# Earlier weight loads, squares by rows, contiguous weights and tokens, and later value products in a one-layer attention trunk

## The chip, the core and the metric

The kernel runs on one core of a Trainium2 chip. Its engines work in parallel, each through its own instructions in order: PE (TensorE, matrix products; PEld is its weight load), ACT (ScalarE), DVE (VectorE), POOL (GpSimd) and SP (SyncE), which here only issues transfers. All transfers of the program go through SP's one queue and are carried out by 16 DMA engines. The metric is device time in microseconds (us) of one execution.

## The reference, cut to what matters

```python
def project(h, g_norm, w_in, b_f):
    u = rmsnorm(h, g_norm) @ w_in              # 1024 -> 4104 columns
    qa, ka, va, ga, qb, kb, vb, gb, fl = jnp.split(u, ...)   # 512 each, fl 8
    logf = log_sigmoid(fl + b_f)
...
# heads A (8): stick-breaking attention      heads B (8): softmax with a forgetting decay
#   w = sigmoid(z) * prod of later sigmoid(-z)      p = softmax(q k / 8 + c_q - c_k)
mixed = concat([oa * silu(ga), ob * silu(gb)])
h = h + mixed @ w_out;   y = rmsnorm(h, final_g)
```

There are 2048 prompt tokens, 16 meta tokens before them and 32 tokens of a running stream (2096 rows of 1024), whose 32 tokens also attend to a cache of 2048 keys. Keys, values and log forgets are outputs too. All is float32.

## The kernel before

Products keep float32 precision by splitting each factor into a high and a low part (ACT copies the high part, `sub` or a multiply-subtract makes the low one on DVE, or on POOL for streamed tokens) and adding three products (`mm3`, L261 to L263). A projection is cut into **sections** of 512 columns: `v1`, `k1`, `q1` for heads B, then `k0`, `v0`, `q0`, `g0` for heads A and the gates, `g1`, and the two halves of the output product (`ob`, `oa`). A section has two **units** of 256 columns (`load_unit`): each is loaded in two halves of 512 KB into raw tiles (`wraw`, `wraw2`), then split into `whi`, `wlo`, eight row blocks a unit. A unit's steps (loads, splits) lie in a list `prep`, from which `tick` takes one at a time while a section's products are written down (`every` 2: at every second tick).

The time line has three stages. **First**, v1, k1 and q1 run alone on PE from tokens that stay resident. `feed` brings the 17 blocks of 128 tokens (transposed, `x_T`, 512 KB), splits them and finds each token's norm: ACT squares the block, POOL adds the squares in three instructions, a PE product sums over partitions (`ptx`, `root`), and `newton` (DVE, ACT) makes `r_all`, by which v1's results `vt` are scaled. 40 products without use (`WARM`) run before the weights are there. **Second**, attention of heads B (`fx_main`) is interleaved with a filler: k0, v0, q0, g0, then g1 and the output products. There tokens are streamed a chunk at a time (`stream`: load `xw` from `x_K`, copy, subtract on POOL), the next chunk during the current one, at the ticks. **Third**, attention of heads A (`sb_main`): per step a score tile (`a`, ACT sigmoids, a DVE scan, a POOL product), for an earlier step four transposes `pta` on PE copied by ACT to `pth`, and after four of them the eight value products `four_pv` (`pv_half`, L701), `poa`. They are put off by one step:

```python
pend.append((t + (1 if f.__name__ == "four_pv" else 2), f))
```

Instructions are written in this order, but a scheduler that plans with costs of its own then orders each engine's queue; only q1's PE and DVE instructions are pinned to the written order. What is printed below is what the diff touches.

Of the kernel before, what the change touches and what calls it, by code (L numbers as in the profile page):

```python
# [16 lines left out]
NX = 2048  # L17
# [34 lines left out]
NW = 9  # L52
FINE = ('k1', 'q1')
# [25 lines left out]
def trunk_step_kernel(ctx, tc, x_all, x_T, x_K, ca_kT, ca_v, cb_kT, cb_v, cb_lfT, norm_g, w_in, b_f, w_out,  # L79
# [77 lines left out]
    def constants():  # L157
        mf = stage("mf", F32, "sg")[:, :SEC]
        dma(mf, mask_c)
        nc.vector.tensor_copy(masks16, mf)  # L160
        sf = stage("sf", F32, "sg")
# [8 lines left out]
        one = stage("one", F32, "sg")[0:8, :SEC]  # L170
# [6 lines left out]
    def load_unit(src, cols, kt, nm, g=None, raw1=None):  # L177

        hi = w_p.tile([128, KT * 264], F32R, tag="whi", name=f"whi{nm}")
        lo = w_p.tile([128, KT * 264], F32R, tag="wlo", name=f"wlo{nm}")  # L180
        hi, lo = ([a[:, k * cols:(k + 1) * cols] for k in range(kt)] for a in (hi, lo))
        raw = {}

        def load(i):
            if i and raw1 is not None:
                raw[i] = raw1
# [10 lines left out]
        def split(i, ks=range(kt // 2)):  # L197
            for k in ks:
# [12 lines left out]
        if nm[:2] in FINE:  # L211
            part = [[lambda i=i: load(i)] + [lambda: None] * NOP + [lambda i=i, k=k: split(i, (k, k + 1)) for k in (0, 2)]
                    for i in range(2)]
            return (hi, lo), part[0] + part[1]
        return (hi, lo), [lambda: load(0), lambda: split(0), lambda: load(1), lambda: split(1)]
# [17 lines left out]
    class Units:  # L233
        every = 2
# [3 lines left out]

        def prepare(self, u):
            un, steps = self.unit(u)  # L240
            self.un.append(un)
            self.prep += steps
# [37 lines left out]
    class SecT(Units):  # L280
        def __init__(self, nm, base, chunks, src, acc, evac, ahead=None, lead=0):
            super().__init__()
            self.nm, self.base, self.chunks, self.src, self.acc, self.evac = nm, base, chunks, src, acc, evac
            self.ahead, self.lead = ahead, lead
            self.every = 1 if lead else 2
# [3 lines left out]
        def unit(self, u):  # L289
            b = self.base + 256 * u  # L290
            return load_unit([w_in[:, b:b + 256]], 256, KT, f"{self.nm}{u}", g_col)
# [5 lines left out]
        def run(self):  # L297
# [13 lines left out]
            for c, (a, n, us) in enumerate(seq):  # L311
# [8 lines left out]
                for i, (p, b, m) in enumerate(order):  # L320
                    if self.next and c == half and i == len(order) // 2:
# [55 lines left out]
    class SecV(Units):  # L377
        def __init__(self, s, chunks, src, acc):
            super().__init__()
            self.s, self.chunks, self.src, self.acc, self.raw1 = s, chunks, src, acc, None  # L380
            self.next = None

        def unit(self, u):
            s = self.s
            base = SECS * s + 2 * SEC
            cols = [w_in[:, base + 256 * u:base + 256 * u + 256]]
            if s and u == 0:
                cols.append(w_in[:, 2 * SECS:2 * SECS + 8])
            return load_unit(cols, 264 if s and u == 0 else 256, KT, f"v{s}{u}", g_col, self.raw1 if u == 0 else None)
# [23 lines left out]
        def run(self):  # L413
# [9 lines left out]
            for i, (a, n) in enumerate(chunks):  # L423
# [10 lines left out]
                for j, (t, u) in enumerate(order):  # L434
                    if self.next and i + 1 == len(chunks) and j == len(ts):
# [169 lines left out]
    def stream(nm, a, n):  # L605
        t = {}
        eng = nc.gpsimd
        n0 = n if n <= XC else 256
# [34 lines left out]
        if n0 < n:  # L643
            steps += halve(lambda: raw(1), lambda: part("xh", 1), lambda: part("xl", 1), pairs(KT, KT), eng)
# [7 lines left out]
        def at_(tag):  # L652
            return lambda k, c, m: (part(tag)[:, k, c - a:c - a + m] if c - a < n0 else
                                    part(tag, 1)[:, k, c - a - n0:c - a - n0 + m])
# [132 lines left out]
    class SbSet:  # L787
# [40 lines left out]
        def b(self, i):  # L828
# [13 lines left out]
            wt = f2k("pth", f"pth{gr.nm}_{kc}_{j}", 4)  # L842
# [170 lines left out]
    def sb_main():  # L1013
# [45 lines left out]
        while t < len(first_a) or second:  # L1059
# [280 lines left out]
    def out_b():  # L1340
# [17 lines left out]
        for j, c in enumerate(seq):  # L1358
# [12 lines left out]
            for i, ((a, r, mh, ml), u) in enumerate(order):  # L1371
                if j == 0 and i == len(order) // 2:
                    ob.ready()
                if j == 4 and i == len(order) // 2:
# [68 lines left out]
    k0 = SecT("k0", SEC, CH_K, stream, ps_a, evac_k(0))  # L1443
# [311 lines left out]
```

## Time and profile before

| | |
|---|---|
| median of 3 runs | 1927.68 us (1919.27 to 1928.73) |
| the profiled execution's own time | 1933.34 us |
| its span, first to last instruction | 1931.3 us |
| PE busy | 1871.1 us, 97% |
| DVE, POOL, ACT busy | 1268.2, 1142.8, 1052.9 us |
| mean granted TensorE clock | 0.985 |
| transfers | 330.69 MB, 171 GB/s |

The span is what the profile divides into busy and idle time; the execution's own time is 2.0 us longer, and this execution lay 5.7 us above the median. A PE that is idle waits for data; a PE that is busy at a granted clock of 0.5 works at half speed (1.2 of 2.4 GHz).

### The profile page before, as it was taken

The numbers are of one execution on the slowest core, as the hardware profiler recorded it, in microseconds if no ns is written. First come the engines' busy times: TensorE is split into PE (matmuls) and PEld (weight loads), VectorE is DVE, ScalarE is ACT, GpSimd is POOL, SyncE is SP. The second block draws the span as 40 slices with busy tenths as digits, with TensorE's granted clock in tenths as the row PEclk, the third lists the DMA queues.
The fourth block names the chain that finished last, engine by engine and source line by source line (L and its number), as shares of the span: only waits on it lengthen the run. The fifth ranks groups of instructions, "written<-read, shape, count | busy, mean of one in ns | idle before, by whom it ended". The sixth has DMA issues, their size and how long they took to land.

```text
span 1931.3 us, 35966 instructions
## 1 busy us (share of the span) xinstructions
PE 1871.1 (97%) x12154; PEld 1474.2 (76%) x12154; DVE 1268.2 (66%) x2387; ACT 1052.9 (55%) x2291; POOL 1142.8 (59%) x1691
## 2 busy tenths in 40 slices
PE   7999999999999999999999999999998999999998
PEld 6999998676776777767777788777876766766676
DVE  5436336765575445566566467788878897778776
ACT  5541213453454454645355577787766777777742
POOL 3500002786777777767786676667766777667400
PEclk8999999999999999999999999999999999999999
DMA  7656757566566454667667545475656554534454
GB/s 160 186 140 148 182 138 189 146 185 163 165 167 162 123 163 137 189 194 213 202 216 213 180 142 185 139 230 167 207 179 196 169 187 136 165 112 143 154 201 175
DMA packets 260431, 330.69 MB, mean 171 GB/s; under 512 B 46685, under 2 KB 195382, under 8 KB 254102
## 3 DMA queue, kind: packets, MB, share of 16 engines
q1 hardware_dynamic: 260246, 328.39, 57.9%
q8 instruction: 96, 1.57, 0.3%
q14 instruction: 89, 0.73, 0.1%
HBM read 211.61 MB, written 116.68 MB: 170 GB/s over the span
## 4 chain that ended last, share of the span: by engine, by line
PE 76%; DVE 9%; DMA 7%; ACT 3%; issue 2%; POOL 2%; SPq 1%; DVEq 0%; POOLq 0%; ACTq 0%
PE pob L701 6%; PE poa L701 5%; PE pta L840 5%; PE sb L1151 3%; PE psTq L261 3%; PE smb L1123 3%; PE psv L261 3%; PE sb L1152 3%; PE psTq L263 3%; PE psTq L262 3%; PE psTk L261 3%; PE psv L262 3%; PE psv L263 3%; PE psTk L263 3%; PE psTk L262 3%; PE sa L781 3%
## 5 line engine op out<-in xcount | busy, mean ns | idle before, releaser
L753 POOL TENSOR_TENSOR wa<-wa,mba 128x512 f32<-128x512 f32 (+1 forms) x320 | 367.2, 1150 | 153.9 <-DVE wa L747 132.2
L1165 POOL TENSOR_TENSOR accb<-accb,pfb 128x512 f32<-128x512 f32 (+1 forms) x256 | 297.6, 1162 | 122.3 <-ACT pfb L1155 106.5
L747 DVE TENSOR_TENSOR_SCAN wa<-sa,wa,ones_r 128x512 f32<-128x512 f32 x192 | 244.3, 1278 | 48.1 <-ACT sa L744 34.4
L1155 ACT ACTIVATE pfb<-sb 128x512 f32<-128x512 f32 (+1 forms) x320 | 175.2, 552 | 182.8 <-PE sb L1152 175.1
L1131 DVE TENSOR_REDUCE mxb<-smb 128x1 f32<-128x512 f32 (+1 forms) x320 | 195.2, 613 | 101.2 <-PE smb L1123 96.7
L843 ACT COPY ptha<-pta 128x512 f32<-128x512 f32 (+1 forms) x320 | 167.1, 526 | 94.5 <-PE pta L840 91.4
L743 ACT ACTIVATE mba<-sa 128x512 f32<-128x512 f32 (+1 forms) x320 | 174.4, 545 | 20.0 <-POOL wa L753 16.2
L840 PE MATMUL pta<-ident,wa 128*128 128x128 f32 x1088 | 174.2, 275 | 8.5 <-ACT ptx L957 2.6
L744 ACT ACTIVATE sa<-sa 128x512 f32<-128x512 f32 (+1 forms) x320 | 174.1, 544 | 0.0
L840 PEld LDWEIGHTS pta<-ident,wa 128*128 128x128 f32 x1088 | 129.8, 141 | 39.6 <-issue 5.4
L781 PE MATMUL sa<-kca,qaa 128*128 128x512 f32 (+3 forms) x352 | 151.3, 430 | 4.5 <-DVE wa L747 4.5
L701 PE MATMUL poa<-ptha,vca 128*64 128x512 f32 (+2 forms) x640 | 148.7, 554 | 7.1 <-ACT ptha L843 6.7
L701 PE MATMUL pob<-pfb,vcb 128*64 128x512 f32 (+1 forms) x640 | 152.8, 574 | 0.0
L261 PE MATMUL psTg<-xhg,whig 128*128 128x260 f32 x512 | 149.0, 291 | 0.0
L263 PE MATMUL psTg<-xhg,wlog 128*128 128x260 f32 x512 | 145.2, 284 | 0.0
L262 PE MATMUL psTg<-xlg,whig 128*128 128x260 f32 x512 | 144.9, 283 | 0.0
L747 DVE TENSOR_TENSOR_SCAN wa<-sa,ones_r,m 128x512 f32<-128x512 f32 (+3 forms) x128 | 111.8, 878 | 41.6 <-ACT sa L744 24.6
L1123 PE MATMUL smb<-k2b,q2b 66*128 66x512 f32 (+1 forms) x320 | 121.0, 379 | 11.8 <-DVE mxb L1131 6.3
L1151 PE MATMUL sb<-qab,kcb 128*128 128x512 f32 (+1 forms) x320 | 123.6, 386 | 0.7 <-ACT pfb L1155 0.7
L782 PE MATMUL sa<-kca,qz 128*128 128x512 f32 (+3 forms) x352 | 122.3, 360 | 0.0
L1152 PE MATMUL sb<-q2b,k2b 70*128 70x512 f32 (+1 forms) x320 | 120.8, 378 | 0.0
L261 PEld LDWEIGHTS psTg<-xhg,whig 128*128 128x128 f32 x512 | 97.0, 189 | 9.8 <-issue 2.8
(291 smaller groups left out, 5243.2 us busy)
## 6 DMA issues: line engine op xcount, KB each, us to landing
xhg<-x_s SPq DMA_DIRECT2D x16, 1040.0 KB
xlg<-x_s SPq DMA_DIRECT2D x16, 1040.0 KB
xwk<-in_x_K_dram SPq DMA_DIRECT2D x8, 1048.0 KB
k_s<-kx SPq DMA_DIRECT2D x64, 131.0 KB
xwq<-in_x_K_dram SPq DMA_DIRECT2D x8, 1040.0 KB
x_s<-xhq SPq DMA_DIRECT2D x8, 1040.0 KB
x_s<-xlq SPq DMA_DIRECT2D x8, 1040.0 KB
q_s<-q SPq DMA_DIRECT2D x64, 130.0 KB
```

Source lines behind the costliest of these rows:

```text
L261: nc.tensor.matmul(out, a_h[k], b_h[k], start=(k == 0), stop=False)
L262: nc.tensor.matmul(out, a_h[k], b_l[k], start=False, stop=False)
L263: nc.tensor.matmul(out, a_l[k], b_h[k], start=False, stop=(k == n - 1))
L701: nc.tensor.matmul(po[64 * side:64 * side + 64, :n], v, p[:, :n], start=first, stop=False)
L747: nc.vector.tensor_tensor_scan(out=w[:, 1:n + 1], data0=ps[:, :n], data1=m01[:, :n] if diag else ones_t[:, 0:1].broadcast_to([128, n]), in ...
L753: nc.gpsimd.tensor_tensor(w[:, :n], w[:, :n], take[:, :n], ALU.mult)
L781: nc.tensor.matmul(out, self.qa[:, bs], k, start=True, stop=False)
L840: nc.tensor.transpose(pt[:, b * 128:b * 128 + 128], self.w[b][:, c:c + 128], ident)
L1123: nc.tensor.matmul(ps[:, :SEC - s0 + m], q2[0:66, bs], k2[0:66, s0:SEC + m], start=True, stop=True)
L1131: nc.vector.tensor_reduce(mx[:, b, kc:kc + 1], ps[:, v0:v0 + nv + m], AX.X, ALU.max)
L1151: nc.tensor.matmul(ps[:, :n], hd.k[kc][:, js], self.qa[:, :n], start=True, stop=False)
L1165: nc.gpsimd.tensor_tensor(self.acc[:, :n], self.acc[:, :n], pf[:, :n], ALU.add)
```

## The change

- Weights are laid out on the host as one array `w_K`, unit after unit, so that a half unit is one contiguous run of 4 KB a partition (it was 1 KB pieces of a row of `w_in`, and for v1's first unit 32-byte pieces besides). Tokens of the streamed sections are laid out per chunk (`x_K`, `x_V`, `x_Q`) in the same way: 8.4 KB runs where pieces of 1 KB were.
- For sections in `TWO` both units' parts are made by `fetch` when the section before begins its last chunk: the first unit's two loads go out there, the second unit's loads follow when the first unit's half is split. Splits go one row block a tick (`every` 1) where they went two at every second tick.
- In `feed` the squares come from rows: each block is loaded a second time, as rows (`x_all`, 2 x 256 KB), and ACT squares it with a sum along the row (`accum_out`). POOL's additions and the PE products `ptx` are gone; `newton` runs for several blocks at once (`ROOTS`). Raw blocks lie in two kinds of tiles, four in all. The lead before v1 is 4.0 blocks (3.5), and 16 unused products run (40).
- v0's 2096 tokens are cut into eight chunks of 256 and one of 48, which is the fifth (before: seven of 256 and a last one of 304).
- `four_pv` is put off by two steps, with six `pth` tiles (four).

```diff
+NP = 6
-NL = 3.5
-LAG = 2
+NL = 4.0
+NA = 2.0
+ROOTS = (0, 2, 4, 7, 10, 13, 15, 16)
-WARM = 40
+WARM = 16
-CH_V = [(c * 256, 256) for c in range(7)] + [(1792, 304)]
+CH_V = [(c * 256, 256) for c in range(8)]
+CH_V.insert(4, (NX, NS + NM))
...
-            r3 = raw[i][:, :kt // 2 * cols].rearrange("p (k c) -> p k c", k=kt // 2)
-            c = 0
-            for a in src:
-                w = a.shape[1]
-                dma(r3[:, :, c:c + w], a.rearrange("(i k p) c -> i p k c", p=128, i=2)[i])
-                c += w
+            n = kt // 2 * cols
+            dma(raw[i][:, :n], w_K[:, W_AT[nm] + i * n:W_AT[nm] + i * n + n])
...
-            return (hi, lo), [lambda: load(0), lambda: load(1), lambda: None] + [
-                lambda i=i, k=k: split(i, range(k, k + kt // 4)) for i in range(2) for k in range(0, kt // 2, kt // 4)]
+            return (hi, lo), [lambda: load(0), lambda: load(1)], [
+                lambda i=i, k=k: split(i, (k,)) for i in range(2) for k in range(kt // 2)]
...
+        def fetch(self):
+
+            if self.two and not self.un:
+                self.parts = [self.unit(u) for u in range(2)]
+                self.un = [x[0] for x in self.parts]
+                for f in self.parts[0][1]:
+                    f()
...
+            self.fetch()
+            steps = self.parts[u][2]
+            if u == 0:
+
+                h = len(steps) // 2
+                for i, f in ((h, self.parts[1][1][0]), (2 * h, self.parts[1][1][1])):
+                    steps[i - 1] = lambda a=steps[i - 1], f=f: (a(), f())
             self.prep += steps
...
-            self.every = 1 if lead else 2
+            self.two = nm in TWO
+            self.every = 1 if lead or self.two else 2
...
+                    if self.next and c == half and i == 0:
+                        self.next.fetch()
...
-            dma(t["xw"][:, :KT * n].rearrange("p (k t) -> p k t", k=KT), x_K[:, :, a:a + n])
+            x = {"k": x_K, "v": x_V, "q": x_Q}[nm[0]]
+            dma(t["xw"][:, :KT * n], x[:, KT * a:KT * a + KT * n])
...
-            wt = f2k("pth", f"pth{gr.nm}_{kc}_{j}", 4)
+            wt = f2k("pth", f"pth{gr.nm}_{kc}_{j}", NP)
...
-                    pend.append((t + (1 if f.__name__ == "four_pv" else 2), f))
+                    pend.append((t + 2, f))
...
+            def fetch(t):
+
+                rows[t] = [stage(f"xrow{t}_{i}", F32, "sg")[:rows_of(t), :SEC] for i in range(2)]
+                for i in range(2):
+                    dma(rows[t][i], x_all[t * 128:t * 128 + rows_of(t), i * SEC:i * SEC + SEC])
+
+            def squares(t):
+                for i, x in enumerate(rows.pop(t)):
+                    nc.scalar.activation(x, x, AF.Square, accum_out=ss[:rows_of(t), i, t:t + 1])
+                if t + 1 < NT:
+                    fetch(t + 1)
+                if t in ROOTS:
+                    todo.append(slice(rooted[-1] + 1 if rooted else 0, t + 1))
+
+            def root():
+                while todo:
+                    c = todo.pop()
+                    nc.vector.tensor_tensor(ss[:, 0, c], ss[:, 0, c], ss[:, 1, c], ALU.add)
+                    newton(v[:, 0, c], r_all[:, c], v[:, 1, c], ss[:, 0, c])
+                    rooted.extend(range(c.start, c.stop))
...
-                sq = [stage(f"sq{t}_{i}", F32, "sg")[:, :4 * r] for i in range(2)]
-                for i in range(2):
-                    nc.scalar.activation(sq[i].rearrange("p (k c) -> p k c", k=4), raw[:, 4 * i:4 * i + 4], AF.Square)
-                nc.gpsimd.tensor_tensor(sq[0], sq[0], sq[1], ALU.add)
-                nc.gpsimd.tensor_tensor(sq[0][:, :2 * r], sq[0][:, :2 * r], sq[0][:, 2 * r:], ALU.add)
-                out = n_p.tile([128, 128], F32, tag="ss", name=f"ss{t}", bufs=3)[:, :r]
-                nc.gpsimd.tensor_tensor(out, sq[0][:, :r], sq[0][:, r:2 * r], ALU.add)
+                if t == 0:
+                    yield 0.0
+                if t == 0:
+                    fetch(0)
+                else:
+                    squares(t - 1)
                 yield HB
-                if len(todo) > LAG:
-                    todo.pop(0)()
-
-                def root(t=t, r=r, ss=out):
-                    pt = ps_t.tile([128, SEC], F32, tag="pt", name=f"ptx{t}")
-                    nc.tensor.matmul(pt[:r, 0:1], ss, ones_t[:, 0:1], start=True, stop=True)
...
+                root()
```

## Rows read from the trace of the kernel before

**Rows 1.** The page: busy time of each engine, its share and instructions.
```profile
PE 1871.1 (97%) x12154; PEld 1474.2 (76%) x12154; DVE 1268.2 (66%) x2387; ACT 1052.9 (55%) x2291; POOL 1142.8 (59%) x1691
```

**Rows 2.** Stretches: us, busy PE PEld DVE ACT POOL (instructions), PE clock, DMA share, GB/s.
```profile
12.31:132.29 119.98, 109.55 (x852) 107.55 (x851) 57.01 (x152) 61.76 (x139) 47.88 (x49) 0.93 0.63 173
320.00:360.00 40.00, 35.66 (x172) 27.12 (x172) 30.79 (x59) 17.05 (x36) 22.39 (x30) 0.87 0.59 145
...
575.00:595.00 20.00, 17.56 (x110) 11.41 (x110) 13.15 (x21) 9.75 (x22) 14.09 (x11) 0.83 0.74 158
...
815.00:835.00 20.00, 17.94 (x104) 12.24 (x105) 16.99 (x32) 10.30 (x25) 15.78 (x14) 0.92 0.71 226
...
1440.00:1490.00 50.00, 43.66 (x305) 32.76 (x304) 38.15 (x62) 31.30 (x70) 33.74 (x65) 0.97 0.62 193
```

**Rows 3.** Waits of PE up to 132.29 us: total us, times, longest.
```profile
PE psv L261 <- ACT whiv L204: 6.4, 3, 3.3
PE ptx L1516 <- POOL ss L1509: 3.3, 2, 3.1
```

**Rows 4.** Timeline of ACT at the start: start us, us, instruction, idle before it.
```profile
4.23 1.04 ACT L1501 CAST xh<-xraw 128x1024 fp32r<-128x1024 f32 x1 [1.93 <-DMA xraw<-in_x_T_dram]
...
12.25 1.73 ACT L204 ACTIVATE whiv<-wrawv,g_col 128x264 fp32r<-128x264 f32 x4 [5.92 <-DMA wrawv<-in_w_in_dram]
17.81 1.74 ACT L204 ACTIVATE whiv<-raw,g_col 128x264 fp32r<-128x264 f32 x4 [3.83 <-DMA raw<-in_w_in_dram]
```

**Rows 5.** Timeline of PE: the unused products, and k1's first.
```profile
1.56 10.92 PE L1546 MATMUL warm<-masks 128*128 128x512 bf16 x40 [1.56 <-DVE masks L142]
...
132.29 0.34 PE L261 MATMUL psTk<-xh,whik 128*128 128x384 f32 x1
```

**Rows 6.** Stretches, as in Rows 2: two of weight loads, one of tokens, steady v1.
```profile
7.00:9.00 2.00, 2.00 (x11) 0.90 (x10) 0.00 (x0) 0.00 (x0) 1.84 (x3) 1.00 0.79 85
27.00:29.00 2.00, 2.00 (x11) 2.00 (x11) 1.84 (x1) 0.63 (x1) 1.92 (x2) 0.50 1.00 122
38.00:39.00 1.00, 0.00 (x0) 0.00 (x0) 0.58 (x1) 0.16 (x1) 1.00 (x1) 1.00 0.93 369
60.00:100.00 40.00, 39.37 (x330) 39.26 (x330) 21.45 (x46) 25.07 (x53) 27.44 (x27) 1.00 0.64 195
```

**Rows 7.** Groups by line up to 132.2 us: busy us, mean ns, idle before.
```profile
L1505 ACT ACTIVATE sq<-xraw 128x512 f32<-128x512 f32 x32 | 19.7, 628 | 16.5 <-POOL ss L1509 10.1 <-POOL sq L1506 5.8 <-DVE rs L571 0.6
...
L1516 PE MATMUL ptx<-ones_r,ss 128*128 128x1 f32 x32 | 4.9, 228 | 3.3 <-POOL ss L1509 3.3
```

**Rows 8.** Timelines of SP and ACT: a token block from issue to its copy.
```profile
82.37 0.37 SPq L89 DMA_DIRECT2D xraw<-in_x_T_dram  x1
...
83.28 0.43 SPq L89 DMA_DIRECT2D v_s<-vt  x1
...
86.28 1.05 ACT L1501 CAST xh<-xraw 128x1024 fp32r<-128x1024 f32 x1 [1.56 <-DMA xraw<-in_x_T_dram]
```

**Rows 9.** The chain that ended last, its longest pieces: start, us, what.
```profile
335.52 9.90 DMA wrawk<-in_w_in_dram
...
419.10 7.64 DMA xwk<-in_x_K_dram
```

**Rows 10.** Line 205 in 344 to 356 us: ns min/median/max.
```profile
L205 DVE SCALAR_TENSOR_TENSOR wlok<-wrawk,g_col,whik x8: 471/1487/1524, 345.8 to 353.9; 128x256 fp32r<-128x256 f32 x8
```

**Rows 11.** Waits of PE in the whole trace.
```profile
PE poa L701 <- ACT ptha L843: 6.7, 4, 2.0
```

**Rows 12.** Timeline around one such wait.
```profile
1450.10 0.69 DVE L1309 TENSOR_TENSOR oa<-oa,gfa 128x512 f32<-128x512 f32 x1 [3.68 <-DMA gfa<-gf_s]
...
1451.98 1.59 PE L701 MATMUL poa<-ptha,vca 128*64 128x512 f32 x3 [1.97 <-ACT ptha L843]
```

**Rows 13.** Tile xwv, v0's token chunks: ns min/median/max, first and last start.
```profile
L92 POOL TENSOR_TENSOR xlv<-xwv,xhv x32: 1273/1302/1719, 546.1 to 754.7; 128x512 fp32r<-128x512 f32 x32
L89 SPq DMA_DIRECT2D xwv<-in_x_K_dram x8: 588/603/625, 525.6 to 728.2; - x8
```

More of the change, by code (lines that the diff above doesn't have):

```diff
@@ L78, in trunk_step_kernel @@
 @with_exitstack
-def trunk_step_kernel(ctx, tc, x_all, x_T, x_K, ca_kT, ca_v, cb_kT, cb_v, cb_lfT, norm_g, w_in, b_f, w_out,
+def trunk_step_kernel(ctx, tc, x_all, x_T, x_K, x_V, x_Q, ca_kT, ca_v, cb_kT, cb_v, cb_lfT, norm_g, w_K, b_f,
                       final_g, ident_c, mask_c, smask_c, rows_c, pick_c,
@@ L169, in constants @@
         dma(den_s[:, NX:TQ], ones_t[0:8, :NS])
-        one = stage("one", F32, "sg")[0:8, :SEC]
+        one = stage("one", F32, "kt")[0:8, :SEC]
         nc.gpsimd.memset(one, 1.0)
@@ L174, in constants, with load_unit, place @@
             dma(kb_s[:, 130:134, c:c + n], one[:, :n].unsqueeze(1).broadcast_to([8, 4, n]))
[L177 to L181, printed above, removed]
+    def load_unit(cols, kt, nm, g=None, raw1=None):
+        hi, lo = [], []
         raw = {}
+        def place():
+            for x, tag in ((hi, "whi"), (lo, "wlo")):
+                a = w_p.tile([128, KT * 264], F32R, tag=tag, name=f"{tag}{nm}")
+                x.extend(a[:, k * cols:(k + 1) * cols] for k in range(kt))
         def load(i):
             if i and raw1 is not None:
-                raw[i] = raw1
+                raw[i] = raw1()
             else:
@@ L214, in load_unit @@
             return (hi, lo), part[0] + part[1]
+        place()
         return (hi, lo), [lambda: load(0), lambda: split(0), lambda: load(1), lambda: split(1)]
@@ L233, in trunk_step_kernel @@
     class Units:
-        every = 2
+        every, two = 2, False
         def __init__(self):
             self.un, self.prep, self.xs, self.ticks = [], [], None, 0
-        def prepare(self, u):
-            un, steps = self.unit(u)
-            self.un.append(un)
+        def fetch(self):
[4 more added lines that the diff above has]
+                    f()
+        def prepare(self, u):
+            if not self.two:
+                un, steps = self.unit(u)
+                self.un.append(un)
+                self.prep += steps
+                return
+            self.fetch()
[4 more added lines that the diff above has]
+                    steps[i - 1] = lambda a=steps[i - 1], f=f: (a(), f())
             self.prep += steps
@@ L289, in unit @@
         def unit(self, u):
[L290 to L291 removed]
+            return load_unit(256, KT, f"{self.nm}{u}", g_col)
         def first_x(self):
@@ L381, in __init__ @@
             self.next = None
+            self.two = f"v{s}" in TWO
+            self.every = 1 if self.two else 2
         def unit(self, u):
             s = self.s
[L385 to L389, printed above, removed]
+            return load_unit(264 if s and u == 0 else 256, KT, f"v{s}{u}", g_col, self.raw1)
         def first_x(self):
@@ L434, in run @@
                 for j, (t, u) in enumerate(order):
+                    if self.next and i + 1 == len(chunks) and j == 0:
+                        self.next.fetch()
                     if self.next and i + 1 == len(chunks) and j == len(ts):
@@ L1373, in out_b @@
                     ob.ready()
+                if j == 4 and i == 0:
+                    oa.fetch()
                 if j == 4 and i == len(order) // 2:
@@ L1708 @@
     blocks = [x_all[t * 128:t * 128 + 128].reshape(-1, KT, 128).transpose(2, 1, 0).reshape(128, -1) for t in range(NT)]
+    w_in, w_out = a["w_in"][0], a["w_out"][0]
+    units = {f"{x}{u}": w_in[:, c + 256 * u:c + 256 * u + 256] for x, c in COLS.items() for u in range(2)}
+    units["v10"] = _np.concatenate([units["v10"], w_in[:, 2 * SECS:2 * SECS + 8]], axis=1)
+    units.update({f"o{s}{u}": w_out[SEC * s:SEC * s + SEC, SEC * u:SEC * u + SEC] for s in range(2) for u in range(2)})
+    units = _np.concatenate([units[n].reshape(-1, 128, units[n].shape[1]).transpose(1, 0, 2).reshape(128, -1)
+                             for n in W_AT], axis=1)
     ins = {
@@ L1718 @@
         "norm_g": a["norm_g"].reshape(KT, 128).T,
-        "w_in": a["w_in"][0],
+        "w_K": units,
         "b_f": a["b_f"],
-        "w_out": a["w_out"][0],
         "final_g": a["final_g"],
```

84 lines of the change are left out of this document (50 added, 34 removed).

## The prediction

> **What bounds the kernel now.** I began with the page. PE is busy for 97% of the span and no other engine for more than 66% [rows 1]: time can only be won where PE idles, works at half speed, or does work that falls away. So the next view is the stretches, read for two things: the stretch less PE's busy time, and the PE clock. A mean clock of 0.93 over 120 us says that PE was at half speed for 0.07 x 120 x 2 us and lost half of it, 8.4 us. Read in this way [rows 2], the first stage (12.31 to 132.29) lost 10.4 idle + 8.4 = 18.8 us; 320 to 360 (from q1 to k0) 4.3 + 5.2 = 9.5; 575 to 595 (into v0) 2.4 + 3.4 = 5.8; 815 to 835 (into q0) 2.1 + 1.6 = 3.7; and 1440 to 1490 (heads A) 6.3 + 1.5 = 7.8. These 45.6 us are what the change can reach; elsewhere I found little to win. Then the waits say what PE waited for: in the first stage for split weights (6.4) and the squares' sums (3.3) [rows 3].
>
> **The start.** ACT copies the first token block at 4.23, but the first weights only at 12.25, and their second half at 17.81 [rows 4]. PE's unused products cover the time to 12.48 [rows 5], so the first useful product runs near 12.8, when the first of four copies is done. Why so late? While weights alone come in, the DMA engines are busy for 0.79 to 1.00 of the time and move only 85 to 122 GB/s; while token blocks come in, in 4 KB runs, they move 369 GB/s at 0.93 [rows 6]. The pieces of `w_in` (1 KB, 16 KB apart) cost three to four times what contiguous bytes cost.
>
> A rule of the Trainium skill speaks against the change here: "DMA: Bandwidth & Descriptors", Specifications, has transfers at line rate from 512 bytes on. By it the 1 KB pieces are at line rate already and longer runs buy nothing, which is the third case below; the 85 and 122 GB/s disagree with it.
>
> Laid out as `w_K`, the two halves (0.54 MB each) should move at about 305 GB/s, which is what steady v1's 195 GB/s at a share of 0.64 makes at full share [rows 6]. They follow the token block that was there at 4.2: 4.2 + 1.8 = 6.0 and 7.8. With the first copy PE starts near 7.0. Sixteen unused products at the mean of 0.27 us end near 6, so PE is free then. The terms:
>
> - PE starts at 7.0, not 12.8: +5.8. Bounds: 0 (weights land as before) and 6.8.
> - The waits for weights and sums, 6.4 + 3.3 [rows 3]: +9.7. Bounds 0 and 9.7.
> - The 34 `ptx` products are 4.9 us busy [rows 7], overlapped with their neighbours: +2.4, bounds 0 and 4.9. POOL's additions free an engine that PE doesn't wait for otherwise: 0.
> - Of the 8.4 us of half speed, which follow those waits, I take 3.3 back; bounds 0 and 8.4.
> - New waits: block 1 now comes behind 1.1 MB of weights and block 0's rows, 2.1 MB after the first block: 4.2 + 6.9 = 11.1, a copy (1.05) and a subtraction of like size, 13.3. PE needs it near 9.9. With a little for the second unit's weights, -4.4; bounds 0 and -10.
> - The rows. Each block now brings 0.5 MB of tokens, 0.5 MB of rows and 0.5 MB of results (1.57 MB). PE needs (132.3 - 12.8 - 18.8 - 2.4)/17 = 5.8 us a block, so 271 GB/s against 305: just enough. But rows have one pair of tiles: the next block's rows go out only after this block's are squared. A block takes 3.9 us from issue to copy [rows 8] and two squares 1.26 [rows 7], 5.2 us in all; with a block copy ahead of them on ACT (1.05) 6.2; with four result stores at 0.4 and a token load (0.37) before the next issue on SP as well, 8.2. `newton`, hence the results, hence PE's accumulators, wait for it. I take 6.2 (the copy is surely there; the scheduler can set ready stores aside): 16 x 0.4 = -6.4. Bounds 0 and 16 x 2.4 = -38.4.
>
> Together 21.2 - 10.8 = **10.4 us** faster; v1 ends near 122, not 132.3.
>
> **Section switches.** Into k0, the second unit's load was issued at 335.5 and took 9.9 us to land [rows 9]; then DVE split eight row blocks at a median of 1.49 us, where an undisturbed one takes 0.47 [rows 10], and PE stood by. The change issues that load once the first unit's half is split, most of a chunk earlier; into v0 and q0 it is the same. The 19.0 us of the three switches are the upper bound. The split work itself stays, 16 instructions a unit on ACT and DVE, and DVE still also serves PE's row maxima; in pieces of one block it holds them up half as long. I take 8: about half at k0, a third at the others. Lower bound 0. The loads now go out ahead of a chunk's tokens on SP; a 1 MB token chunk landed in 7.6 us [rows 9] and has a whole chunk's time, so 0 for that; the shorter DMA time of contiguous tokens is hidden too, and if chunks were late it would be a small gain.
>
> **Value products.** PE waited 6.7 us for `ptha` in four places [rows 11]; one shows why: DVE sat 3.68 us on a transfer, ACT behind it, and the copy of the transposes came late [rows 12]. A further step (1.3 us of planned work in the code) lies between copy and product, so waits of 1.5 to 2.0 us shrink but need not go; with the half speed after them (1.5) 8.2 us are to be had. I take 4; bounds 0 and 8.2. Queued behind the later products is only the next group's, and two more tiles carry the copies: 0.
>
> **The chunk of 48.** It has two products' groups, about 5.8 us of filler, in place of 11.6; chunks of 256 started 28.9 us apart ((728.2 - 525.6)/7), so this one lasts near 14 us. In its 8 ticks the next chunk's steps (11 ticks) don't all fit. Issue at 3.5, landing 7.6, four POOL subtractions at 1.3 [rows 13]: the last is there at 16.3, over 2 us late. I take -1.5; bounds 0 and -6.
>
> **Sum.** 10.4 + 8 + 4 - 1.5 = 20.9 us off the profiled execution's 1933.3, 1912.4. That execution lay 5.7 above the median of the runs shown; against the median, 1927.7 - 20.9 = **1907**. Runs of before lie within 9.5 us; 0.5% (9.6 us) is about what a measurement can tell from no change.
>
> **The rivals.**
>
> 1. The forecast, 1895 to 1915 by its own terms: 0.50.
> 2. All terms near their good bounds: start 19, switches 15, values 8, chunk 0 make 42: **1886**. For it: each lost stretch has its wait named in the trace. Against: half of the waits in 320 to 360 are behind other DVE work. 0.13.
> 3. Contiguity buys nothing and the start stays bound by bytes: the earlier start and the weights' waits fall out, the saved `ptx` go into rows, start 0, the rest 10.5: **1917**. For it: 8.6 MB more to load. Against: 369 GB/s. 0.17.
> 4. The waits only move: DVE and ACT stay as late in heads A (value products 0), splits hold up other maxima (0), the chunk of 48 costs 6; 10.4 - 6 = 4.4: **1923**. For it: the transfer of rows 12 is untouched. 0.12.
> 5. The other side: squares by rows set v1's pace. At 8.2 us a block the start is 21.2 - 4.4 - 38.4 = -21.6, with 10.5 from the rest -11.1: **1939**. It eats all gains from 7.5 us a block on and is slower by 0.5% from 8.1. For it: SP issues in order, one pair of row tiles. Against: 5.2 us when nothing is in the way. 0.08.
>
> Faster by over 0.5% (under 1918): nearly all of the first, the second, over half of the third, 0.71. Within 0.5%: the fourth and the remainders, 0.21. Slower: 0.08. The range leaves out the slow end of the fifth case and the fast half of the second: 1887 to 1929.
>
> **What would show it.** In the profile after: the first copy of weights on ACT near 6 us and k1's first product near 122; the DMA share near 0.9 in v1; no `psv <- whiv` among PE's waits; `wrawk` of the second unit issued before 330; fewer us in `poa <- ptha`; one late chunk in v0. The prediction is wrong if squares or `r_all` head PE's or ACT's waits in v1, if the clock falls to 0.5 more often than before, or if another wait of DVE fills the gaps around 350, 580 and 1450.

## The result, and the profile after

The changed kernel takes **1907.06 us** (median of five executions, 1906.55 to 1911.02), the kernel before 1924.55 (five, 1919.27 to 1928.73): a ratio of 0.9903, 95% interval 0.9884 to 0.9921. The forecast was 1907, faster. The profiled execution took 1911.02 us with a span of 1909.3, so the two profiles lie 22.0 us apart, the medians 17.5. As will be seen, the sum came out while half of its terms did not.

The page of after, engines (busy us, share of the span, instructions):

```profile
PE 1846.9 (97%) x12096; PEld 1456.9 (76%) x12096; DVE 1252.1 (66%) x2342; ACT 1051.0 (55%) x2317; POOL 1089.1 (57%) x1643
```

PE is still the bound; the 24 us less busy time against [rows 1] are fewer unused products, no `ptx`, and less work at half speed. Where the 22 us came from is read from one kind of landmark, the start of each section's first product on PE's timeline:

| execution | v1 | k1 | q1 | k0 | v0 | q0 | g0 | heads A | last products | PE's end |
|---|---|---|---|---|---|---|---|---|---|---|
| before | 12.8 | 132.3 | 227.0 | 318.0 | 578.3 | 816.8 | 1046.5 | 1080.3 | 1827.4 | 1923.7 |
| after | 7.8 | 130.3 | 223.9 | 318.1 | 560.5 | 794.2 | 1019.8 | 1053.5 | 1804.0 | 1901.6 |
| lead of after | 5.0 | 2.0 | 3.1 | -0.1 | 17.8 | 22.6 | 26.7 | 26.8 | 23.4 | 22.1 |

At k0's first product nothing is left of the start's gain. k0 gains 17.9, v0 4.8, q0 4.1; heads A and the last products give 4.7 back. The stretches that answer to [rows 2] (v1; q1 to k0; the rest of k0, which [rows 2] don't hold; into v0; into q0; the waits in heads A). Columns as there:

```profile
7.80:130.32 122.52, 106.48 (x817) 104.44 (x818) 40.23 (x106) 66.35 (x165) 0.52 (x1) 0.93 0.76 241
311.50:350.00 38.50, 34.74 (x205) 27.02 (x205) 29.81 (x64) 15.84 (x33) 20.78 (x29) 1.00 0.64 180
350.00:540.00 190.00, 189.25 (x1279) 140.54 (x1277) 115.88 (x242) 91.65 (x197) 148.76 (x143) 1.00 0.61 177
540.00:580.00 40.00, 38.19 (x265) 27.89 (x264) 29.65 (x63) 22.14 (x50) 28.20 (x27) 1.00 0.65 194
785.00:815.00 30.00, 28.50 (x200) 21.22 (x199) 24.09 (x45) 18.01 (x42) 21.95 (x22) 1.00 0.69 223
1415.00:1465.00 50.00, 45.67 (x325) 35.38 (x324) 40.23 (x66) 32.33 (x73) 33.90 (x69) 0.93 0.68 199
```

v1 now idles for 16.0 us and its clock is 0.93 as before. In the next four stretches the clock is 1.00. 190.0 us of k0 do what took 198.9 before (the stretch 359.0 to 557.9; the same 1279 products):

```profile
359.00:557.90 198.90, 193.60 (x1279) 143.57 (x1277) 119.28 (x242) 91.40 (x197) 147.93 (x142) 0.98 0.62 168
```

**The start.** ACT's timeline after, against [rows 4]: the first weights are copied at 7.23, the second half at 8.88, no longer at 12.25 and 17.81.

```profile
4.44 1.05 ACT L1562 CAST xh<-xraw 128x1024 fp32r<-128x1024 f32 x1 [2.13 <-DMA xraw<-in_x_T_dram]
7.23 1.74 ACT L215 ACTIVATE whiv<-wrawv,g_col 128x264 fp32r<-128x264 f32 x4 [1.75 <-DMA wrawv<-in_w_K_dram]
8.88 1.72 ACT L215 ACTIVATE whiv<-wraw,g_col 128x264 fp32r<-128x264 f32 x4
```

The transfers behind it, and steady v1 (the last two columns are DMA share and GB/s). From 4.2 to 6.2 us only weights come in (every packet in the trace is one of their 4.2 KB runs), at 308 GB/s, where [rows 6] have 85 and 122 for pieces:

```profile
4.20:6.20 2.00, 2.00 (x6) 0.65 (x5) 0.68 (x1) 1.05 (x1) 0.00 (x0) 1.00 0.94 308
...
60.00:90.00 30.00, 30.00 (x254) 30.00 (x253) 8.76 (x15) 19.55 (x47) 0.00 (x0) 1.00 0.91 297
```

In 60 to 90 PE is never idle: the loads of rows did not set the pace. But PE's waits up to k1, against [rows 3], have two new heads:

```profile
PE psv L292 <- ACT vt L430: 6.8, 2, 6.1
PE ptr L1576 <- issue: 4.2, 1, 4.2
PE psv L292 <- ACT xh L1562: 2.9, 2, 1.7
PE psv L292 <- ACT fl L432: 1.6, 1, 1.6
```

`whiv` and `ptx` are gone from the list, as forecast. The 6.1 us are a chain. PE stops at 35.7 for an accumulator, which ACT frees at 41.28 by writing `vt`. ACT waited for DVE's copy of `pick`, one of the constants; that came behind the mask, for whose transfer DVE sat 5.36 us. DVE's timeline, then ACT's and PE's:

```profile
39.23 0.43 DVE L170 CAST masks<-mf 128x512 bf16<-128x512 f32 x1 [5.36 <-DMA mf<-in_mask_c_dram]
...
40.99 0.21 DVE L177 CAST pick<-sf 8x128 fp32r<-8x128 f32 x1
```

```profile
41.28 0.47 ACT L430 ACTIVATE vt<-psv,r_all 128x256 f32<-128x256 f32 x1 [1.72 <-DVE pick L177]
```

```profile
41.81 0.58 PE L292 MATMUL psv<-whiv,xh 128*128 128x256 f32 x1 [6.14 <-ACT vt L430]
```

The link in this trace is one word of the diff, in a line that the cut above leaves out: the pieces of the constants lie in tiles tagged `kt` (they were `sg`), and `vt` takes its tiles from the same two.

```diff
-        mf = stage("mf", F32, "sg")[:, :SEC]
+        mf = stage("mf", F32, "kt")[:, :SEC]
```

The 4.2 us are PE's order: `ptr`, the transposition of all norms, stood some 200 products ahead of v1's end, and the last block's norm was ready at 104.5. PE's timeline, then DVE's:

```profile
104.62 0.27 PE L1576 MATMUL ptr<-ident,r_all 128*17 128x128 f32 x1 [4.17 <-issue]
```

```profile
104.36 0.16 DVE L606 TENSOR_TENSOR r_all<-r_all,rs 128x1 f32<-128x1 f32 x1
```

**k0.** What PE waited for between 440 and 525 before (first fence) is not in the list after, where one wait is left in all of 350 to 540 (second fence):

```profile
PE smb L1123 <- DMA q2b<-q_s: 2.9, 1, 2.9
PE smb L1123 <- DMA k2b<-kb_s: 1.6, 1, 1.6
```

```profile
PE ptmb L1169 <- DVE mxb L1136: 0.8, 1, 0.8
```

`q2b` and `k2b` are small transfers for the scores of heads B. SP's timeline before shows why one was late: `q2b` was issued at 463.70 behind a chunk of tokens and half a unit of weights, and its reader ran at 473.14.

```profile
460.24 0.59 SPq L89 DMA_DIRECT2D xwk<-in_x_K_dram  x1
...
461.59 0.42 SPq L89 DMA_DIRECT2D wrawv<-in_w_in_dram  x1
...
463.70 0.64 SPq L89 DMA_DIRECT2D q2b<-q_s  x1
```

The same order stands after (450.51, 451.39, 453.39). Only what is ahead moves faster, and of the two loads it is the weights. Before, the tokens' pieces moved at 316 GB/s and the weights' pieces behind them at 83 (first fence; the two are told apart by the sizes of the packets). After, the half unit of weights falls into a stretch of 393 GB/s (second fence).

```profile
462.00:466.00 4.00, 4.00 (x37) 2.17 (x36) 3.25 (x7) 1.20 (x2) 3.84 (x5) 1.00 0.99 316
466.50:470.00 3.50, 3.50 (x31) 3.46 (x29) 2.08 (x5) 1.74 (x4) 1.16 (x3) 1.00 0.77 83
```

```profile
455.00:457.00 2.00, 2.00 (x28) 1.28 (x25) 0.85 (x2) 0.00 (x0) 1.84 (x3) 1.00 1.02 393
```

With k0's products counted off in both traces, 4.6 of the 8.9 us are won at this wait and 3.4 at the one for `k2b`, each with the half speed behind it. `k2b`, issued at 497.29, had a chunk of tokens ahead (494.87) and no weights, and those pieces moved at 335 GB/s from 497 to 500; what took that wait away is not shown.

**Switches.** The two halves of k0's second unit go out at 313.00 and 317.19 (the second at 335.52 before, [rows 9]); SP's timeline after:

```profile
313.00 0.39 SPq L99 DMA_DIRECT2D wrawk<-in_w_K_dram  x1
...
317.19 1.99 SPq L99 DMA_DIRECT2D wrawk<-in_w_K_dram  x1
```

**Heads A.** The waits of `poa` for `ptha` [rows 11] are gone. In their place, PE's waits from 1053 to 1804, with a 3.2 us wait at 1424, where one of [rows 12] was:

```profile
PE sa L811 <- DVE wa L777: 6.0, 8, 1.4
PE pta_m L887 <- ACT ptha L873: 5.1, 3, 3.2
PE pta L870 <- ACT ptha L873: 3.8, 5, 1.5
```

### The profile page after: what moved, and what is told of

Same layout as the page of the kernel before. It is cut to its first block, busy times and chain, and to the rows that moved or that the text cites. A ratio compares the mean times of both kernels' runs of the same rounds, so it can differ in the third digit from the quotient of the medians.

```text
span 1909.3 us, 35868 instructions
## 1 busy us (share of the span) xinstructions
PE 1846.9 (97%) x12096; PEld 1456.9 (76%) x12096; DVE 1252.1 (66%) x2342; ACT 1051.0 (55%) x2317; POOL 1089.1 (57%) x1643
## 4 chain that ended last, share of the span: by engine, by line
PE 76%; DVE 8%; DMA 6%; ACT 4%; issue 3%; POOL 1%; SPq 1%; DVEq 0%; ACTq 0%; POOLq 0%
PE pob L731 7%; PE poa L731 5%; PE pta L870 4%; PE sb L1181 3%; PE psTk L292 3%; PE sb L1182 3%; PE smb L1153 3%; PE psv L292 3%; PE psTk L294 3%; PE psTk L293 3%; PE psTq L292 3%; PE psv L294 3%; PE psv L293 3%; PE psTq L293 3%; PE psTq L294 3%
## 5 line engine op out<-in xcount | busy, mean ns | idle before, releaser
L777 DVE TENSOR_TENSOR_SCAN wa<-sa,wa,ones_r 128x512 f32<-128x512 f32 x192 | 244.5, 1279 | 47.1 <-ACT sa L774 29.5
L731 PE MATMUL pob<-pfb,vcb 128*64 128x512 f32 (+1 forms) x640 | 148.2, 563 | 0.0
L731 PE MATMUL poa<-ptha,vca 128*64 128x512 f32 (+2 forms) x640 | 144.4, 562 | 0.0
L1153 PE MATMUL smb<-k2b,q2b 66*128 66x512 f32 (+1 forms) x320 | 119.5, 373 | 4.9 <-DVE mxb L1161 4.1
```

The lines of the kernel that those rows point to most:

```text
L731: nc.tensor.matmul(po[64 * side:64 * side + 64, :n], v, p[:, :n], start=first, stop=False)
L777: nc.vector.tensor_tensor_scan(out=w[:, 1:n + 1], data0=ps[:, :n], data1=m01[:, :n] if diag else ones_t[:, 0:1].broadcast_to([128, n]), in ...
L1153: nc.tensor.matmul(ps[:, :SEC - s0 + m], q2[0:66, bs], k2[0:66, s0:SEC + m], start=True, stop=True)
```

## The experiments

They ran on two chips (e1 to e8 on one, e9 to e12 on the other). On both the kernel before took 1930 us, and ratios are to that kernel beside them. The landmarks are those of the table above, from one profiled execution of each.

| run | median us | ratio, 95% | v1 | k1 | q1 | k0 | v0 | q0 | heads A | last | end |
|---|---|---|---|---|---|---|---|---|---|---|---|
| e12 changed, again | 1911.14 | 0.9904 (0.9886 to 0.9922) | 8.1 | 124.8 | 218.4 | 313.1 | 557.1 | 790.7 | 1050.1 | 1803.3 | 1900.9 |
| e1 start | 1911.78 | 0.9894 (0.9875 to 0.9913) | 7.4 | 122.4 | 215.9 | 310.5 | 555.0 | 788.7 | 1048.1 | 1805.0 | 1902.6 |
| e2 old switch | 1919.67 | 0.9947 (0.9928 to 0.9965) | 6.7 | 129.5 | 223.2 | 314.1 | 561.2 | 799.1 | 1061.4 | 1812.8 | 1910.4 |
| e3 strided tokens | 1918.33 | 0.9930 (0.9911 to 0.9950) | 7.1 | 126.5 | 220.1 | 314.3 | 558.5 | 793.8 | 1053.2 | 1803.8 | 1901.2 |
| e4 early values | 1911.62 | 0.9904 (0.9886 to 0.9921) | 7.1 | 130.3 | 223.9 | 318.6 | 561.3 | 795.0 | 1054.2 | 1801.1 | 1901.6 |
| e5 constants late | 1902.96 | 0.9856 (0.9831 to 0.9881) | 7.5 | 115.7 | 214.0 | 308.5 | 552.0 | 787.5 | 1047.7 | 1797.8 | 1895.4 |
| e6 layout alone | 1915.00 | 0.9918 (0.9898 to 0.9938) | 12.9 | 124.7 | 218.4 | 309.3 | 558.8 | 798.3 | 1061.4 | 1809.1 | 1905.3 |
| e7 strided both | 1939.02 | 1.0047 (1.0028 to 1.0066) | 13.1 | 140.6 | 234.9 | 330.2 | 582.5 | 818.5 | 1080.2 | 1832.4 | 1929.6 |
| e8 old squares | 1914.95 | 0.9920 (0.9901 to 0.9940) | 7.2 | 134.0 | 227.6 | 321.3 | 564.5 | 798.9 | 1059.7 | 1808.5 | 1905.9 |
| e9 constants in k1 | 1897.62 | 0.9835 (0.9814 to 0.9855) | 7.3 | 114.4 | 208.0 | 302.7 | 545.4 | 779.1 | 1038.4 | 1789.3 | 1886.7 |
| e10 early values | 1896.35 | 0.9826 (0.9805 to 0.9847) | 7.1 | 114.6 | 208.3 | 302.4 | 547.3 | 780.9 | 1040.3 | 1788.5 | 1888.7 |
| e11 chunk of 304 | 1919.76 | 0.9944 (0.9922 to 0.9966) | 7.1 | 130.2 | 223.8 | 318.2 | 561.6 | 796.3 | 1066.3 | 1813.6 | 1911.4 |

**e12, the changed kernel again.**

> The changed kernel once more, beside the others on their chip. Theory: ratio 0.989 to 0.992; the waits of vt behind the constants (6 us) and of ptr (3 to 6 us) are there again, so they belong to the kernel and not to one execution; heads A's length differs by up to 5 us from the first profile's 750.5, which is then what single executions differ by.

The same ratio. `vt` waited 6.2 us at 34.6 again; `ptr` waited 1.4 us here, 4.2 in the first profile, 2.8 and 5.8 in e3 and e4, which have the same order there. So k1 begins anywhere from 124.8 to 130.3 with the same code, and a lead of 2.0 us is the low end of 2.0 to 7.5 (of the kernel before there is only one trace). Heads A took 753.2 us.

**e6, the layout alone** (the kernel before, with `w_K`, `x_K`, `x_V`, `x_Q` and its own order of everything):

```diff
-            r3 = raw[i][:, :kt // 2 * cols].rearrange("p (k c) -> p k c", k=kt // 2)
...
+            n = kt // 2 * cols
+            dma(raw[i][:, :n], w_K[:, W_AT[nm] + i * n:W_AT[nm] + i * n + n])
...
-            dma(t["xw"][:, :KT * n].rearrange("p (k t) -> p k t", k=KT), x_K[:, :, a:a + n])
+            x = {"k": x_K, "v": x_V, "q": x_Q}[nm[0]]
+            dma(t["xw"][:, :KT * n], x[:, KT * a:KT * a + KT * n])
```

> The kernel before with contiguous weights and tokens and nothing else. Theory: the layout is worth the waits of k0's small transfers (8.9 us of the gain between 350 and 540) and the waits for v1's weights (6.4 us), while the unused products hold PE to 11 and the switches stay as they are: ratio 0.991 to 0.993. Rival: the gain is made by the order of loads and splits, and the layout alone is worth 5 us or less: ratio 0.997 or more. A third possibility: shorter transfers also shorten the switches, ratio under 0.989.

0.9918: five sixths of the whole change's gain (0.82 of 0.97%). k1 begins 7.6 us earlier than before, k0 is 10.8 us shorter (249.5 against 260.3), the wait for `whiv` is 3.9 us, and of the small transfers 0.6 us is left:

```profile
PE smb L1123 <- DMA k2b<-kb_s: 0.6, 1, 0.6
```

ACT copies the first weights at 7.29; the first product stays at 12.9, since 40 unused products hold PE until then.

**e7, the old layout of both, in the changed order.**

```diff
-            n = kt // 2 * cols
-            dma(raw[i][:, :n], w_K[:, W_AT[nm] + i * n:W_AT[nm] + i * n + n])
+            r3 = raw[i][:, :kt // 2 * cols].rearrange("p (k c) -> p k c", k=kt // 2)
...
-            dma(t["xw"][:, :KT * n], x[:, KT * a:KT * a + KT * n])
+            dma(t["xw"][:, :KT * n].rearrange("p (k t) -> p k t", k=KT), x_K[:, :, a:a + n])
```

> The changed kernel with the old layout of both, weights and tokens in pieces of 1 KB, its order of loads and splits kept. Theory: it loses what strided tokens lose (e3: 6 us) and 5 to 9 us in v1, where PE begins near 13 and waits for whiv; ratio 0.996 to 0.999. Rival: contiguous weights buy nothing once loads go out earlier, ratio 0.992 to 0.994 as in e3. If k0's profile falls on one of the longer executions, smb waits for q2b or k2b between 440 and 530.

1.0047, slower than before and beyond both expectations: without the layout, the rest of the change loses. The first weights crawl as before, at 85 GB/s with the DMA engines 0.99 busy:

```profile
9.00:11.00 2.00, 0.00 (x0) 0.00 (x0) 0.00 (x0) 0.00 (x0) 0.00 (x0) 0.84 0.99 85
```

k1 begins 10.3 us later than after. In k0 (252.3 us, against 242.4) the small transfers are late again, PE's waits from 440 to 530:

```profile
PE smb L1161 <- DMA kcb<-kb_s: 4.2, 1, 4.2
PE smb L1161 <- DMA k2b<-kb_s: 0.8, 1, 0.8
```

**e3, the old layout of tokens only** (the second half of that diff).

> The changed kernel with the streamed tokens read as before, in pieces of 1 KB (192 bytes for the chunk of 48), weights contiguous. Theory: k0 won 8.9 us because a chunk's transfer no longer holds up the small transfers behind it in the queue (before, scores waited 2.9 us for q2b and 1.6 for k2b, with 6.8 us of half speed behind); so these waits come back between 440 and 520 and the median is about 1916. Rival: those waits were an accident of one execution or came from the weights in the same queue: 1905 to 1909, no wait of smb for q2b or k2b.

0.9930 against 0.9904, about 5 us, with intervals that overlap. The profiled execution took 1910.68 us where the other five took 1917.26 to 1920.02. In its trace the tokens come in pieces again, and yet nothing waits for `q2b`, and `smb` waits only 0.5 us for `k2b`: with contiguous weights the queue is not held up. So this trace speaks against the theory, which laid k0's gain to the tokens. What the five longer executions lost is not recorded. Against e7, which has the weights in pieces too, e3 is 1.2% better: most of the layout's worth lies in the weights.

**e2, the old switches.**

```diff
-            return (hi, lo), [lambda: load(0), lambda: load(1)], [
-                lambda i=i, k=k: split(i, (k,)) for i in range(2) for k in range(kt // 2)]
+            place()
+            return (hi, lo), [lambda: load(0), lambda: load(1), lambda: None] + [
+                lambda i=i, k=k: split(i, range(k, k + kt // 4)) for i in range(2) for k in range(0, kt // 2, kt // 4)]
...
-            self.two = nm in TWO
-            self.every = 1 if lead or self.two else 2
+            self.every = 1 if lead else 2
```

> The changed kernel with the section switches as before: no fetch at the last chunk, splits of two row blocks at every second tick, second unit's load after the first unit's splits; weights and tokens stay contiguous. Theory: the order of loads and splits made the switches shorter (6.6 us into k0, 4.0 into v0, 2.3 into q0), so they come back: 1907.1 + 12.9 = 1920, at least 1915, and heads A's end shifts with it. Rival: contiguous weights alone made them shorter, since a half unit lands sooner: 1905 to 1910, and the wait for row maxima at 350 stays short.

0.9947: 0.43%, or 8.3 us lost, where the theory had 12.9. Some comes back: k0 begins 4.0 us earlier than after (the splits no longer stand in q1's last chunk), then k0 is 4.7 us longer, v0 4.2 and the way from q0 to heads A 3.0. The wait for row maxima into v0 is 3.0 us (e2, first fence) against 1.1 (after, second fence), both from 545 to 580:

```profile
PE smb L1151 <- DVE mxb L1159: 3.0, 2, 2.7
```

```profile
PE smb L1153 <- DVE mxb L1161: 1.1, 1, 1.1
```

**e8, squares as before.** `squares`, `fetch` and `root` of the changed kernel give way to:

```diff
+                sq = [stage(f"sq{t}_{i}", F32, "sg")[:, :4 * r] for i in range(2)]
...
+                nc.gpsimd.tensor_tensor(sq[0], sq[0], sq[1], ALU.add)
...
+                    nc.tensor.matmul(pt[:r, 0:1], ss, ones_t[:, 0:1], start=True, stop=True)
```

> The changed kernel with squares, POOL's additions and the products ptx as before; loads, constants and everything else as changed. Theory: rows cost v1 nothing in pace (it ran at 5.9 us per block with them, as before) and save ptx and the wait for it, so going back loses 2.4 to 5.7 us: ratio 0.9915 to 0.9935, k1 begins at 132 to 136. Rival: the rows' 8.6 MB and the late last block cost more than ptx, so k1 begins before 128 and the ratio is under 0.989.

k1 begins at 134.0 (after 130.3, e12 124.8), and PE waits 8.8 us in `ptx`:

```profile
PE ptx L1554 <- POOL ss L1547: 6.2, 4, 3.2
PE ptx L1554 <- DVE smasks L176: 2.6, 1, 2.6
```

That is the theory's side, but the intervals of the two ratios, 0.9920 and 0.9904, overlap.

**e1, constants in a tile of their own, `ptr` behind v1.**

```diff
-        mf = stage("mf", F32, "kt")[:, :SEC]
+        mf = pool.tile([128, SEC], F32, tag="cn", name="mf", bufs=1)
...
         ng.drain()
+        norms()
         n_es.close()
```

> The changed kernel with the constants' three pieces in a tile of their own (not in the two tiles of the results vt) and with the transposition ptr behind v1's last product (it stood in PE's order 220 products ahead of it). Theory: the start won 2.0 us in place of 10.4 because two waits were added, vt behind the constants (6.1 us idle, 9.3 us of the gain lost up to 54 us with the half speed behind it) and ptr behind the last block's norm (4.2 us idle, 4.8 lost). Without them k1 begins at 116, not 130.3, and the median is 1907.1 - 14.1 = 1893. Rival: rows and tokens pace v1 anyway, so other waits for tokens, rows or results fill the gaps and k1 still begins at 127 or later; median 1903 or more.

Mostly wrong. k1 begins at 122.4, 8 us earlier than in the first profile but only 2.4 earlier than in e12. 6.6 us of waits for `vt` are left, and SP's timeline shows why, the constants hold up the queue itself: from one block of tokens to the next it takes 14 us.

```profile
32.45 0.42 SPq L99 DMA_DIRECT2D xraw<-in_x_T_dram  x1
...
34.92 0.33 SPq L99 DMA_DIRECT2D xrow<-in_x_all_dram  x1
39.29 0.33 SPq L99 DMA_DIRECT2D sf<-in_smask_c_dram  x1
...
42.78 3.88 SPq L99 DMA_DIRECT2D kb_s<-one  x5
46.71 1.24 SPq L99 DMA_DIRECT2D xraw<-in_x_T_dram  x1
```

Heads A took 756.9 us in this execution (after 750.5), in the same order of PE's instructions; the median shows no gain. So the name of the tile was not all of it: with a tile of their own the constants still cost v1 these waits.

**e5, constants behind v1** (`norms` holds the transposition `ptr` and the store of its row; tiles as in the changed kernel):

```diff
-                if t == 6:
-                    constants()
...
         ng.drain()
+        norms()
+        constants()
         n_es.close()
```

> The changed kernel with the constants and the transposition ptr behind v1's last product. Theory: in e1 the constants still held up the queue that issues transfers (the next token block went out at 46.7, 14.3 us after the one before, and PE waited 2.4 and 4.2 us for vt near 42 and 51); out of the way of v1 they cost nothing, k1 begins at 116 (after: 130.3, e1: 122.4), and unless it is given back later the ratio to before is 0.983. Rival: rows and tokens can't come any faster, so k1 begins at 121 or later, ratio 0.987 or more. In either case heads A may take back some us, as in e1 (6 us there, in the same order of PE's instructions).

k1 at 115.7, as the theory had it, ratio 0.9856: 9 us better than the change. 5 us of the lead went in k1, where PE waited 2.8 us for `kf`.

**e9, the same with the constants' transfers written behind the norms' rows, and the constants in the two tiles of the squares' rows** (`sg` again).

```diff
             dma(xroot[c], r_row[:, a:a + n].broadcast_to([128, n]))
+        constants()
         mark("k1")
```

> As e5, but the constants lie in the two tiles of the squares' rows (free by then), and their transfers go out behind those of the norms' rows. Theory: in e5 the 14.6 us won up to k1 shrank to 9.9 at q1, since k1's first result waited for the norms' row behind the ones of the constants in SP's queue (issued at 125.2, first kf at 135.4); with that out of the way q1 begins at 209.5 to 212 (e5: 214.0, after: 223.9), ratio 0.982 to 0.984. Rival: k1's results are late for another reason (the scan of the forget sums on DVE), so q1 begins at 214 and the ratio is 0.9856 as in e5.

On SP's timeline the mask still goes out at 113.24, ahead of the norms' rows (119.83); the five transfers of ones now come behind them (122.10). q1 begins at 208.0, ratio 0.9835. v1 takes 107.1 us (119.5 before) and idles for 5.1 of them:

```profile
7.30:114.40 107.10, 102.02 (x817) 101.03 (x818) 39.25 (x101) 66.31 (x165) 0.00 (x0) 0.97 0.82 260
```

**e4 and e10, early value products** (from the changed kernel and from e9).

```diff
-NP = 6
+NP = 4
...
-                    pend.append((t + 2, f))
+                    pend.append((t + (1 if f.__name__ == "four_pv" else 2), f))
```

> The changed kernel with the value products put off by one step and four pth tiles, as before. Theory: a further step between copy and product only moves the waits, from poa to pta and pta_m (heads A lasted 750.5 us after, 747.2 before); so heads A gets about 3 us shorter or stays, median 1903 to 1907, and the waits of poa for ptha are back. Rival, the term of the prediction: the later products are worth 4 us, median 1911.

> As e9, with value products put off by one step and four pth tiles, as before the change. Theory (from e4: 0.9904 against 0.9903): the step makes no difference, ratio within 0.002 of e9. Rival: early values are better, heads A being 3 us shorter in e4's trace, ratio lower than e9 by 0.002 or more; or the prediction's term, higher by 0.002.

0.9904 against 0.9904 (e12), 0.9826 against 0.9835: no difference either way. In e4's trace `poa` waits for `ptha` again, from 1415 to 1470:

```profile
PE poa L731 <- ACT ptha L873: 4.8, 3, 2.9
```

Heads A took 746.9 us in e4, 748.2 in e10, against 750.5, 753.2 and 750.9 in after, e12 and e9. All traces fall apart this way: 746.9 to 748.2 us in the five with early products (before, e4, e6, e10, e11), 748.8 to 756.9 in the nine with late ones. So late products cost heads A some 3 us. But in e4 and e10 the last products give it back: 100.4 and 100.1 us to PE's end, against 97.6, 97.6 and 97.4 in after, e12 and e9. Why they do is not shown.

**e11, v0's chunks as before** (with early values, whose fewer tiles leave the room; to be set against e4).

```diff
-CH_V = [(c * 256, 256) for c in range(8)]
-CH_V.insert(4, (NX, NS + NM))
+CH_V = [(c * 256, 256) for c in range(7)] + [(1792, 304)]
```

> As e4 (the changed kernel with early values), with v0's chunks as before: seven of 256 and a last one of 304. Theory: the chunk of 48 costs and gains nothing, since PE waits for no tokens in v0 either way (idle under 0.1 us between 580 and 785 after); ratio 0.989 to 0.992 as e4's 0.9904. Rival, the prediction's term: undoing it wins 1.5 us; or, since v0's inside was 1.5 us shorter after, it loses 1.5: neither is beyond the interval, so the trace of 555 to 815 decides, and a chunk of 304 with two more products' groups at its end may move the switch to q0.

Neither: 0.9944 against 0.9904 (e4, and e12 on the same chip as e11), 7.7 us slower. v0 is 1.0 us longer than in e4 and the way from q0 to heads A 10.8, and the row maxima are late as q0 begins (e11 from 785 to 830, then after from 785 to 815):

```profile
PE smb L1156 <- DVE mxb L1164: 5.4, 2, 4.0
```

```profile
PE smb L1153 <- DVE mxb L1161: 0.5, 1, 0.5
```

## Why the number was right and half of its terms were not

The forecast took 20.9 us off the profiled execution; 22.0 came off. Against the medians it is 17.5 us, because this execution of before lay farther above its median than that of after did. And the 1907 was reached from a median of 1927.7, which came out 3.1 us lower over five executions: the hit to the microsecond is luck. Term by term:

- **PE's start, +5.8: right,** +5.0. The rate was the step that mattered, and contiguous weights did move at 308 GB/s, where the sum had 305. Rival 3, that contiguity buys nothing, is refuted from both sides: alone it is worth 0.82% (e6), and taken out of the changed kernel it costs 1.4% (1.0047 over 0.9904). The Trainium skill's "DMA: Bandwidth & Descriptors", Specifications, with line rate from 512 bytes on, does not hold for the weights' pieces of 1 KB (85 GB/s in e7, at a share of 0.99), though tokens' pieces of that length moved 316 in the trace of before; I had put 0.17 on the case that goes by it.
- **Waits for weights and sums, +9.7: right.** Neither is left in the list.
- **The row chain, -6.4: failed.** I took 6.2 us for a block. Between 60 and 90 PE has no idle time at all, and e8 shows that without rows v1 is longer, not shorter. Rival 5 falls with it.
- **The step that failed at the start is the list of new waits.** I priced tokens (-4.4; PE's waits for `xh`, `xl` and `fl` are 5.0) and left out two that the whole diff shows: the constants' tiles changed from `sg` to `kt`, where results wait for them (and their transfers, in a queue that now carries rows as well, hold up tokens, e1), and `ptr` needs the last norm, which came only 4.4 us earlier than before (104.5, 108.9) while PE came to `ptr` 8.8 us earlier (100.4, 109.2). With the half speed behind them they cost what e9 gets back by moving both: 0.69%, 13 us. So the start won 2.0 us in the profile (7.5 in e12's), not 10.4. And the 3.3 us of half speed did not come back (0.93 over 122.5 us is 8.6 us lost, 8.4 before); they do in e9.
- **Section switches, +8: right in mechanism, and nearly in size.** Counted off by products in the same way, the trace gains 9.1 us as k0 begins, of which 3.2 had been lost just ahead of it, in q1's last chunk, where the earlier splits stand; then 4.1 as v0 begins and 3.0 as q0 begins. Part of this is the layout's: e6 alone gains 3.3 as k0 begins. e2 puts the order of loads and splits at 8.3.
- **The layout's worth inside k0: put at nothing, and that failed.** The tokens' shorter transfer was called hidden, and for tokens that is nearly so: their pieces moved at 316 GB/s as it was, and e3 has 5 us for them, not beyond its interval. The contiguous weights were priced at v1 and at the switches alone. But a half unit in pieces, at 83 GB/s, held up the 128 KB behind it in the one queue, and I looked at the loads' own readers alone. k0 won 8.9 us behind its switch, more than half of it at that wait. The Trainium skill's "DMA: Bandwidth & Descriptors", Queues, rings and completion order, says that a DMA engine takes up the descriptors of one ring in ring order; the trace agrees: `q2b` was read 9.4 us after its issue, with 1.6 MB of tokens and weights ahead.
- **Value products, +4: failed.** Worth nothing in the time (e4, e10), and some 3 us lost in heads A: the wait moved from `poa` to `pta` and `pta_m`. That part of rival 4 was right: ACT's copies are as late as they were, whoever is next in PE's order waits.
- **The chunk of 48, -1.5: failed in sign.** Undone in the changed kernel it costs 7.7 us (e11). I looked for its tokens' lateness, and PE waits for no tokens in v0; the 304 it replaces was the chunk in which the next section's splits lie. Why DVE's maxima are late there for 5.4 us with 304 tokens and 0.5 with 256 was not taken further apart.

So the sum held because errors of both signs met. By section of the profile: the start, 10.4 forecast, had given 2.0 at k1 and nothing at k0; k0 to heads A, 6.5 forecast (8 less 1.5), gave 26.9; heads A, 4 forecast, lost 3.4, and the last products 1.3. The parts as the runs have them, each undone by itself: layout 28 us (tokens 5 of them, e3; the weights 23, e7 against e3), switches 8.3, chunk 7.7, squares about 3 (not beyond its interval), values 0, constants and `ptr` -13. They don't add up to the 18.5 of the whole (0.0096 of 1930), since they share waits: the early loads are good only when the weights come quickly, as e7 shows.

e9 and e10, 0.9835 and 0.9826, are the best versions found: 13 and 15 us better than the change, with intervals apart from its own.

## What to carry to other kernels

- When a big transfer gets shorter, look at what is issued behind it in the same queue, not only at who reads it; and where two big ones stand ahead, read the rate of each.
- A changed tile tag is a changed wait. For each tile that an edit renames, ask who else takes tiles under that name, and which transfer now stands between them. (Giving the constants a tile of their own, in e1, was not enough here: their transfers had to leave v1.)
- Several true mechanisms with wrong sizes can meet the right total; landmarks of equal work in both traces show it at once.

## What the runs showed that was not expected

- Two kinds of 1 KB pieces differ in rate, even one behind the other in one stretch of before: tokens (8.4 KB apart) at 316 GB/s, weights (16 KB apart) at 83. Piece length alone doesn't explain it, and no run here takes apart what else differs. The 32-byte pieces of v1's first unit are not the reason for the 85 GB/s in e7: from 13 to 15 us every packet of that trace has 1024 bytes, and they moved at 78 GB/s with the DMA engines 0.96 busy.
- e3's executions fell into two groups, one at 1910.7 us and five from 1917.3 to 1920.0, and the profiled one was the odd one. A single profile can show the rarer kind.
- In e9 no stretch at half speed is left between 25 and 1216 us, though PE still idles there now and then for up to 1.7 us, and for 2.1 us just ahead of the one at 1216; after the idle times of 6.1 and 4.2 us in v1 of the changed kernel, half speed followed.
